# FFN up projection as seven block products (Strassen's scheme, Winograd's form), FFN in two phases through DRAM

## The chip, the cores and the metric

The kernel runs on one core of one Trainium2 chip. The metric is the device time of one execution in microseconds (us). The engines are TensorE (PE in the profile, its weight loads PEld), VectorE (DVE), ScalarE (ACT), GpSimd (POOL) and SyncE (SP), which here only issues DMAs. Every engine works through its own instructions in order and waits on semaphores for the others.

## The reference, cut to what matters

One layer of a model trunk: 1024 tokens, width 1024, FFN width 2816, all in fp32. The change lies in the gated FFN with its causal convolution of width 3, and in the residual around it:

```
h2 = rmsnorm(x, g_ffn[i])
u = causal_dwconv(h2 @ w_up[i], conv_w[i], conv_b[i])          # w_up: 1024 x 5632
x = x + (jax.nn.gelu(u[..., :D_FF], approximate=True) * u[..., D_FF:]) @ w_down[i]   # 2816 x 1024
ple_gate = jax.nn.sigmoid(rmsnorm(x, g_ple[i]) @ w_ple_gate[i])
x = x + ple_gate * (p[i] @ w_ple_up[i])
```

## The kernel before, in words

Every fp32 operand of a product is split into a high part (fp32r, rounded by a ScalarE cast) and the rest (a VectorE subtraction); `split` does both. A product is then three matmuls: high x high, high x rest, rest x high. Each matmul here multiplies a 128x128 stationary block with 128x512 moving columns.

Mixer output. `wout` multiplies the merged branches with the four column quarters of `w_out` and adds them to the eight 128-token rows of x1 (`self.x1[tb]`, in SBUF). In the loop for quarters 2 and 3, `norm_rows` makes the normed rows and `turn` transposes one (8 transposes of 128x128 in two PSUM banks, each emptied by one cast and one subtraction) into `hT`: `ha` for tokens 0 to 511, `hb` for 512 to 1023, each with a high and a rest tile.

Up projection (`ffn`). For each of 22 blocks f, two 128-column blocks of `w_up` are loaded and split: block f (the gelu half) and block 22 + f (the linear half). `gemmT` multiplies one with one token half: 8 contraction blocks x 3 matmuls. So f costs 2 x 2 x 24 = 96 matmuls. `conv` reads the 128x1024 PSUM result: one ScalarE activation and two VectorE multiply-adds on shifted columns. Then gelu, a product of the halves, and a split into `mh`, `ml`.

Down projection (`down`). After two f, their 256 rows of `w_down` are multiplied with every token row: 12 matmuls per row, in two PSUM tiles `ps` of 128x512 (there are two such buffers), each added into x1 by VectorE. This work lies between the up projections of the next f. The last three f are multiplied in the loop that also norms x1 for the last gate (`ple`).

The program fixes the order in which tiles are allocated; a scheduler then sets each engine's order, which is why the orders below are printed from the built programs.

## Time and profile before

| | us |
|---|---|
| median of 3 runs | 1943.54 (1942.53 to 1951.27) |
| the profiled execution | 1945.69 |
| its span, first to last instruction | 1944.0 |
| TensorE busy in the span | 1892.3 (97%) |
| VectorE busy | 1026.9 (53%) |
| ScalarE busy | 686.8 (35%) |
| GpSimd busy | 102.0 (5%) |

The span is the profiled execution without the 1.7 us around it. Busy shares are sums over stages with different limits; a stage is read by its own window, and there by which engine waits for which.

### The profile page before, as it was taken

How to read it: one execution, taken by the hardware profiler on the slowest of the kernel's cores; microseconds unless marked ns; L12 is line 12 of the kernel's file. 1: busy time of each engine (PE TensorE's matmuls, PEld its weight loads, DVE VectorE, ACT ScalarE, POOL GpSimd, SP SyncE). 2: the span in 40 equal slices, each digit the busy share in tenths (PEclk: the TensorE clock that was granted, in tenths of full speed). 3: DMA queues.
4: the chain of work that ended last, by engine and by line, in shares of the span. 5: the costliest groups of instructions: out<-in, count | busy, mean ns of one | idle time of the engine just before them, and what ended most of it. 6: DMA issues, size and time to landing. Idle time of an engine off the chain costs nothing.

```text
span 1944.0 us, 27675 instructions
## 1 busy us (share of the span) xinstructions
PE 1892.3 (97%) x11215; PEld 1550.3 (80%) x11215; DVE 1026.9 (53%) x2193; ACT 686.8 (35%) x1069; POOL 102.0 (5%) x99
## 2 busy tenths in 40 slices
...
GB/s 154 87 152 152 146 133 94 70 75 46 72 32 82 136 118 146 129 133 92 260 169 74 55 55 44 45 43 55 47 35 60 50 49 33 62 26 54 27 148 55
DMA packets 249766, 169.75 MB, mean 87 GB/s; under 512 B 76488, under 2 KB 226718, under 8 KB 249639
## 3 DMA queue, kind: packets, MB, share of 16 engines
...
## 4 chain that ended last, share of the span: by engine, by line
PE 67%; DMA 2%; ACT 1%; DVE 1%; issue 1%; POOL 0%; ACTq 0%; SPq 0%; POOLq 0%; DVEq 0%
PE zt L235 10%; PE zt L236 10%; PE zt L237 10%; PE ps L228 4%; PE ps L227 4%; PE ps L226 4%; PE zt L226 3%; PE zt L227 3%; PE zt L228 3%; PE zt L985 2%; PE zt L987 2%; PE zt L986 1%; PE yps L635 1%; PE yps L648 1%; DMA vr<-in_w_out 1%; PE tr L842 1%
## 5 line engine op out<-in xcount | busy, mean ns | idle before, releaser
L207 DVE TENSOR_TENSOR wl<-wr,wh 128x1024 fp32r<-128x1024 f32 (+1 forms) x78 | 91.0, 1168 | 248.9 <-ACT wh L206 248.5
L235 PE MATMUL zt<-hah,wh 128*128 128x512 f32 (+1 forms) x552 | 219.8, 399 | 0.0
L235 PE MATMUL zt<-hbh,wh 128*128 128x512 f32 (+1 forms) x552 | 218.1, 395 | 0.2 <-ACT hbh L285 0.2
L236 PE MATMUL zt<-hal,wh 128*128 128x512 f32 (+1 forms) x552 | 218.1, 395 | 0.0
L236 PE MATMUL zt<-hbl,wh 128*128 128x512 f32 (+1 forms) x552 | 217.7, 394 | 0.0
L237 PE MATMUL zt<-hbh,wl 128*128 128x512 f32 (+1 forms) x552 | 217.3, 394 | 0.0
L237 PE MATMUL zt<-hah,wl 128*128 128x512 f32 (+1 forms) x552 | 217.0, 393 | 0.0
L206 ACT CAST wh<-wr 128x1024 fp32r<-128x1024 f32 (+1 forms) x87 | 84.2, 970 | 346.3 <-PE zt L236 299.1
L1065 DVE TENSOR_TENSOR x<-x,ps 128x512 f32<-128x512 f32 x154 | 105.3, 686 | 96.0 <-PE ps L228 94.8
L226 PE MATMUL ps<-vh,mh 128*128 128x512 f32 (+1 forms) x334 | 128.7, 385 | 0.2 <-DVE x L1042 0.2
L228 PE MATMUL ps<-vh,ml 128*128 128x512 f32 (+1 forms) x334 | 128.6, 385 | 0.0
L227 PE MATMUL ps<-vl,mh 128*128 128x512 f32 (+1 forms) x334 | 128.5, 385 | 0.0
L235 PEld LDWEIGHTS zt<-hah,wh 128*128 128x128 f32 x552 | 104.6, 190 | 23.8 <-issue 0.5
L235 PEld LDWEIGHTS zt<-hbh,wh 128*128 128x128 f32 x552 | 104.3, 189 | 23.7 <-ACT hbh L285 0.5
L236 PEld LDWEIGHTS zt<-hal,wh 128*128 128x128 f32 x552 | 104.6, 189 | 23.3 <-issue 1.0
L236 PEld LDWEIGHTS zt<-hbl,wh 128*128 128x128 f32 x552 | 104.3, 189 | 23.5 <-DVE hbl L286 0.4
L237 PEld LDWEIGHTS zt<-hah,wl 128*128 128x128 f32 x552 | 104.5, 189 | 23.3 <-issue 0.2
L237 PEld LDWEIGHTS zt<-hbh,wl 128*128 128x128 f32 x552 | 104.5, 189 | 23.1
L206 ACT CAST vh<-vr 128x1024 fp32r<-128x1024 f32 x34 | 34.1, 1047 | 209.3 <-PE ps L228 178.0
L226 PEld LDWEIGHTS ps<-vh,mh 128*128 128x128 f32 x334 | 63.0, 189 | 13.6 <-DVE x L1042 0.4
L227 PEld LDWEIGHTS ps<-vl,mh 128*128 128x128 f32 x334 | 63.0, 189 | 13.4
L228 PEld LDWEIGHTS ps<-vh,ml 128*128 128x128 f32 x334 | 63.0, 188 | 13.3
(395 smaller groups left out, 4073.3 us busy)
## 6 DMA issues: line engine op xcount, KB each, us to landing
wr<-in_w_up SPq DMA_DIRECT2D x44, 512.0 KB
...
wr<-in_w_in ACTq DMA_DIRECT2D x21, 512.0 KB
gwr<-in_w_in ACTq DMA_DIRECT2D x11, 512.0 KB
xt<-in_x SPq DMA_DIRECT2D x8, 512.0 KB
...
fwr<-in_w_in ACTq DMA_DIRECT2D x8, 512.0 KB
```

The lines of the kernel that those rows point to most:

```text
L206: self.nc.scalar.copy(h, r)
L207: eng.tensor_sub(l, r, h.bitcast(F32))
L226: nc.tensor.matmul(ps, lhsT=lh, rhs=rh, start=(i == 0), stop=False)
L227: nc.tensor.matmul(ps, lhsT=lh, rhs=rl, start=False, stop=False)
L228: nc.tensor.matmul(ps, lhsT=ll, rhs=rh, start=False, stop=(i == n - 1))
L235: nc.tensor.matmul(o, lhsT=H[:, k, :], rhs=hh[:, k, :], start=(k == 0), stop=False)
L236: nc.tensor.matmul(o, lhsT=H[:, k, :], rhs=hl[:, k, :], start=False, stop=False)
L237: nc.tensor.matmul(o, lhsT=L[:, k, :], rhs=hh[:, k, :], start=False, stop=(k == NKB - 1))
L635: mm(yps[i][r, o], lhsT=X[r, i, k, :], rhs=main(X, i, X_R)[r], start=True, stop=False)
L985: nc.tensor.matmul(ps[:, cs], lhsT=H[:, k, :], rhs=yh[:, k, cs], start=(k == 0), stop=False)
L987: nc.tensor.matmul(ps[:, cs], lhsT=L[:, k, :], rhs=yh[:, k, cs], start=False, stop=(k == 3))
L1065: self.nc.vector.tensor_add(self.x1[tb][:, cs], self.x1[tb][:, cs], ps)
```

## The change

The up projection of block f is treated as a 2x2 block product. The rows of the left matrix are the gelu block and the linear block (A1., A2.), its columns the lower and the upper 512 of the contraction; the right matrix has the same halves of the contraction as rows and the two token halves as columns (B.1, B.2). Seven products of 12 matmuls take the place of eight. Their operands are sums: s1 = a21 + a22, s2 = s1 - a11, s3 = a11 - a21, s4 = a12 - s2 on the weights (`up_s12`, `up_s3`: four GpSimd operations of 128x512 for each f), and t1 to t4 on the tokens (`up_norm`: four GpSimd operations for each pair of token rows, once). Only token rows 0 to 3 go through `turn`; t1 to t4 and b22 are transposed by `up_turn` (5 x 4 transposes for each pair). The results are put together in SBUF tiles c0 (gelu half) and c1 (linear half) by one copy and seven adds from PSUM, and `up_conv` reads these. x1 is normed in place, after a copy to DRAM (`x1d`). The gated rows go to DRAM (`md`). After all 22 f, x1 is loaded again, and `ffn_down` reads `md` and `w_down` for group after group of two f.

```diff
+    def up_norm(self, p, tmp):
+
+
+        xa, xb = self.x1[p], self.x1[p + 4]
+        lo, hi = slice(0, 512), slice(512, 1024)
+        sub = self.nc.gpsimd.tensor_sub
+        t2 = tmp.tile([P, 512], F32, name="t2", tag="t2", bufs=4)
+        sub(xa[:, lo], xb[:, lo], xa[:, lo])
+        sub(t2, xb[:, hi], xa[:, lo])
+        sub(xb[:, lo], xb[:, hi], xb[:, lo])
+        sub(xa[:, hi], xa[:, hi], t2)
+        return dict(t1=xa[:, lo], t2=t2, t3=xb[:, lo], t4=xa[:, hi], b22=xb[:, hi])
...
+    def up_turn(self, p, rows, pools):
+
+        nc = self.nc
+        ts = slice(p * P, p * P + P)
+        for n, op in enumerate(("t2", "t1", "t3", "t4", "b22")):
+            ps = pools()
+            for k in range(4):
+                nc.tensor.transpose(ps[:, k * P:k * P + P], rows[op][:, k * P:k * P + P], self.ident)
+            p3 = ps[:].rearrange("p (k t) -> p k t", t=P)
+            H, L = self.B[op]
+            nc.scalar.copy(H[:, :, ts], p3)
+            nc.vector.tensor_sub(L[:, :, ts], p3, H[:, :, ts].bitcast(F32))
+            yield 0.44
...
+    def up_s12(self, f):
+
+        r0, r1 = self.raws[f]
+        A, gp = self.A[f], self.nc.gpsimd
+        A["s1"], A["s2"] = self.up_tile("vr")
+        s1, s2, s4 = [self.up.tile([P, 4, P], F32, name=n, tag=n, bufs=1) for n in ("s1r", "s2r", "s4r")]
+        gp.tensor_add(s1, r1[:, 0:4], r1[:, 4:8])
+        gp.tensor_sub(s2, s1, r0[:, 0:4])
+        gp.tensor_sub(s4, r0[:, 4:8], s2)
+        self.sums[f] = s1, s2, s4
...
+    def up_mul(self, ps, f, w, b):
+        nc = self.nc
+        (wh, wl), (bh, bl) = self.A[f][w], self.B[b]
+        for k in range(4):
+            nc.tensor.matmul(ps, lhsT=wh[:, k, :], rhs=bh[:, k, :], start=k == 0, stop=False)
+            nc.tensor.matmul(ps, lhsT=wh[:, k, :], rhs=bl[:, k, :], start=False, stop=False)
+            nc.tensor.matmul(ps, lhsT=wl[:, k, :], rhs=bh[:, k, :], start=False, stop=k == 3)
+            yield 0.7
...
+    def up_m(self, f, c0, u1):
+        nc = self.nc
+        u0 = self.up_conv(c0, f)
+        nc.scalar.activation(u0, u0, AF.Gelu_apprx_tanh)
+        nc.vector.tensor_mul(u0, u0, u1)
+        nc.sync.dma_start(self.md[f], u0)
...
+            m1 = mul(f, "a11", "b11") if f else first[0]
+            nc.scalar.copy(c0[:, lo], m1)
+            if f:
+                u1 = self.up_conv(before[1], NFB + f - 1)
+            else:
+                self.up_load(1)
+            m2 = mul(f, "a12", "b21") if f else first[1]
+            if f:
+                self.up_m(f - 1, before[0], u1)
+                self.up_rest(f)
+            m6 = mul(f, "s2", "t2")
+            add(c0[:, hi], c0[:, lo], m6)
+            add(c0[:, lo], c0[:, lo], m2)
+            if f + 2 < NFB:
+                self.up_load(f + 2)
+            m5 = mul(f, "s1", "t1")
+            if more:
+                self.up_a1(f + 1)
+                self.up_s12(f + 1)
+            else:
+                last()
+            m7 = mul(f, "s3", "t3")
+            add(c1[:, lo], c0[:, hi], m7)
+            add(c1[:, hi], c1[:, lo], m5)
+            add(c0[:, hi], c0[:, hi], m5)
+            if more:
+                self.up_halve(self.A[f + 1]["s2"], self.sums[f + 1][1][:])
+                self.up_halve(self.A[f + 1]["s1"], self.sums[f + 1][0][:])
+            m4 = mul(f, "a22", "t4")
+            add(c1[:, lo], c1[:, lo], m4)
+            m3 = mul(f, "s4", "b22")
+            if more:
+                self.up_s3(f + 1)
+            add(c0[:, hi], c0[:, hi], m3)
+            before = c0, c1
+        u1 = self.up_conv(before[1], 2 * NFB - 1)
+        self.up_m(NFB - 1, before[0], u1)
...
+    def ffn_down(self, ms, pools):
+
+        for g in range(1, NFB // 2):
+            raws = self.down_load(g)
+            for tb in range(NTB):
+                if g == NFB // 2 - 1:
+                    self.down(ms[:1], tb, self.zt.tile([P, T], F32, name="zt", tag="zt") if tb % 2 else None)
                 else:
-                    before = ms
-        return before[1:] + ms
+                    self.down(ms, tb)
+                if tb == 2:
+                    after = self.down_split(g, raws, pools)
+            ms = ms[1:] + after if g == NFB // 2 - 1 else after
+        return ms
...
+
+        def scale(tb):
+            x = self.x1[tb]
+            nc.vector.scalar_tensor_tensor(x, x, scales[tb], g, op0=ALU.mult, op1=ALU.mult)
+        for i in range(NTB + 3):
+            if i < NTB:
+                self.wout(m, 2, W2, order[i], z_tile)
+            if i >= 3:
+                tb = order[i - 3]
+                self.wout(m, 3, W3, tb, z_tile)
+                self.dump("x1", self.x1[tb], tb)
+                scales[tb] = self.rms_scale(self.x1[tb], junk, tmp)
+                nc.sync.dma_start(self.x1d[tb], self.x1[tb])
+            if i >= 4:
+                scale(order[i - 4])
+            if i in (5, 7, 9):
+                self.turn(order[i - 5], self.x1[order[i - 5]], [hT])
+            if i == 5:
+                self.up_a1(0)
+            if i in (6, 8, 10):
+                sums.append(self.up_norm(i // 2 - 3, tmp))
...
+        def norm2():
+            w = self.up_first(junk)
+            self.turn(3, self.x1[3], [hT])
+            next(w)
+            yield 0.88
+            yield from self.up_turn(0, sums[0], t_tile)
+            scale(7)
+            sums.append(self.up_norm(3, tmp))
+            next(w)
+            yield from self.up_turn(1, sums[1], t_tile)
+            next(w)
+            yield from self.up_turn(2, sums[2], t_tile)
+            run(w)
+            yield from self.up_turn(3, sums[3], t_tile)
+        first = [self.pu.tile([P, 512], F32, name="pu", tag="pu") for _ in range(2)]
+        interleave((norm2(), 9.7), (flat([[0.9], self.up_mul(first[0], 0, "a11", "b11"),
+                                          self.up_mul(first[1], 0, "a12", "b21")]), 6.5))
...
+        self.ffn_up(first, lambda: ms.extend(self.down_first(hA)))
+        close_up()
+        close_h2()
+        close_ps()
+        close_ps = self.pools(("ps", 2), ("zt", 3))
+        xp1, _ = self.pool("x1", side="right")
+        self.x1 = [xp1.tile([P, D], F32, name=f"x1_{tb}") for tb in reversed(range(NTB))][::-1]
+        for tb in range(NTB):
+            nc.sync.dma_start(self.x1[tb], self.x1d[tb])
...
+        ms = self.ffn_down(ms, [(hA, "hah"), (hA, "hal"), (hB, "hbh"), (hB, "hbl")])
```

**Order 1.** VectorE, one f of the up projection. Before, for one f: the split of the weights, the two multiply-adds of each half (they read PSUM, `zt`), the product and the split.

```order
L207 TENSOR_TENSOR wl_12044<-wr_12041,wh_12043 128x1024 [waits DMAHW7_49,PE_49,Activation_49]
L1053 SCALAR_TENSOR_TENSOR uc_11964<-zt_11915,par_111,uc_11964 128x1023 [waits Activation_49]
L1054 SCALAR_TENSOR_TENSOR uc_11964<-zt_11915,par_111,uc_11964 128x1022 [waits DVE_49]
L207 TENSOR_TENSOR wl_12231<-wr_12228,wh_12230 128x1024 [waits DMAHW1_49,PE_49,Activation_49]
L1053 SCALAR_TENSOR_TENSOR uc_12023<-zt_11974,par_111,uc_12023 128x1023 [waits Activation_49]
L1054 SCALAR_TENSOR_TENSOR uc_12023<-zt_11974,par_111,uc_12023 128x1022 [waits DVE_49]
L1096 TENSOR_TENSOR uc_11964<-uc_11964,uc_12023 128x1024 [waits DVE_49]
L207 TENSOR_TENSOR ml_12030<-uc_11964,mh_12029 128x1024 [waits Activation_49]
```

In the change, for one f, the stretch from the sixth product (m4) to the product with the linear half; the operations before it are the other adds and the subtractions for s2 and s1.

```order
L1216 TENSOR_TENSOR c1_11611<-c1_11611,pu_11718 128x512 [waits DVE_49,PE_49]
L1100 TENSOR_TENSOR vh_11745<-s3r_11746,vh_11745 128x512 [waits Activation_49]
L1100 TENSOR_TENSOR vh_11745<-rr_11531,vh_11745 128x512 [waits DMAHW5_49,Activation_49]
L1162 SCALAR_TENSOR_TENSOR u_11767<-c1_11611,par_111,u_11767 128x1023 [waits Activation_49]
L1220 TENSOR_TENSOR c0_11610<-c0_11610,pu_11732 128x512 [waits PE_49]
L1163 SCALAR_TENSOR_TENSOR u_11767<-c1_11611,par_111,u_11767 128x1022 [waits DVE_49]
L1100 TENSOR_TENSOR vl_11793<-s4r_11694,vl_11793 128x512 [waits Activation_49]
L1162 SCALAR_TENSOR_TENSOR u_11784<-c0_11610,par_111,u_11784 128x1023 [waits DMAHW2_49,Activation_49]
L1163 SCALAR_TENSOR_TENSOR u_11784<-c0_11610,par_111,u_11784 128x1022 [waits DVE_49]
L1090 TENSOR_TENSOR wl_11970<-rr_11811,wh_11969 128x1024 [waits DMAHW1_49,PE_49,Activation_49]
L1170 TENSOR_TENSOR u_11784<-u_11784,u_11767 128x1024 [waits Activation_49]
L1198 TENSOR_TENSOR c0_11751<-c0_11751,pu_11796 128x512 [waits PE_49]
```

And GpSimd for one f, which had no work in this stage before:

```order
L1108 TENSOR_TENSOR s1r_11692<-rr_11531 128x512 [waits DMAHW5_49,DVE_49]
L1109 TENSOR_TENSOR s2r_11693<-s1r_11692,rr_11529 128x512 [waits DMAHW3_49,Pool_49]
L1119 TENSOR_TENSOR s3r_11746<-rr_11529,rr_11531 128x512 [waits DVE_49]
L1110 TENSOR_TENSOR s4r_11694<-rr_11529,s2r_11693 128x512 [waits DVE_49,Pool_49]
```

What moved: the multiply-adds read SBUF (c1_11611 and c0_11610, the tiles c1 and c0 of this f) instead of PSUM, three subtractions of 128x512 and the one of 128x1024 stand among them, and GpSimd makes four sums beside them.

**Order 2.** VectorE between the loop of `wout` and the first product with a sum. x1_7 is the last row to be finished; `t2l`, `t4l`, `b22l`, `vl` are the rest tiles of the transposed sums, `vr` those of s1 and s2, `vl_10602` that of s4 (from `wh_9994`, made by GpSimd).

```order
L1072 TENSOR_TENSOR b22l_10577<-pu_10640,b22h_10576 128x4x128 [waits Activation_49]
L1072 TENSOR_TENSOR vl_10585<-ps_10623,vh_10584 128x4x128 [waits Activation_49,Pool_49]
L1575 SCALAR_TENSOR_TENSOR x1_7_9522<-x1_7_9522,nst_10548,wl_9992 128x1024 [waits DMAHW3_49,DVE_49]
L1100 TENSOR_TENSOR vr_10603<-wh_9994,vr_10603 128x512 [waits Pool_49]
L1072 TENSOR_TENSOR t2l_10581<-ps_10656,t2h_10580 128x4x128 [waits Activation_49]
L1072 TENSOR_TENSOR t1l_10583<-pu_10666,t1h_10582 128x4x128 [waits Activation_49]
L1072 TENSOR_TENSOR vl_10585<-pu_10673,vh_10584 128x4x128 [waits Activation_49]
L1072 TENSOR_TENSOR t4l_10579<-ps_10680,t4h_10578 128x4x128 [waits Activation_49]
L1072 TENSOR_TENSOR b22l_10577<-pu_10690,b22h_10576 128x4x128 [waits Activation_49]
L1100 TENSOR_TENSOR vr_10603<-wh_9994,vr_10603 128x512 [waits Pool_49]
L1100 TENSOR_TENSOR vl_10602<-wh_9994,vl_10602 128x512 [waits Activation_49]
L1072 TENSOR_TENSOR t2l_10581<-pu_10701,t2h_10580 128x4x128 [waits PE_49]
```

What moved: where `turn` of one row (two subtractions) stood beside 24 matmuls, there are now twenty subtractions for the sums, the scaling of x1_7 in their midst, and the first product that uses a sum (t2) needs the last of the four t2l, seven rows below these.

**Order 3.** SyncE's DMAs. Before, in the middle of the FFN:

```order
L215 DMA vr_12033<-in_w_down 128x2x1024 [waits DMAHW6_49,DVE_49]
L215 DMA wr_11844<-in_w_up 128x8x128 [waits DMAHW1_49,DVE_49]
L215 DMA wr_11909<-in_w_up 128x8x128 [waits DMAHW2_49,DVE_49]
L215 DMA wr_11968<-in_w_up 128x8x128 [waits DMAHW4_49,DVE_49]
L215 DMA wr_12041<-in_w_up 128x8x128 [waits DMAHW5_49,DVE_49]
```

In the change, at the end of the up projection; `u_13863` is the last gated row, `vr` the raw tile of `w_down`, of which there is one.

```order
L1171 DMA md_9999<-u_13754 128x1024 [waits DVE_49]
L1254 DMA vr_13908<-in_w_down 128x2x1024 [waits DMAHW1_49,PE_49]
L1254 DMA vr_14053<-in_w_down 128x2x1024 [waits DMAHW1_49,DVE_49]
L1171 DMA md_9999<-u_13863 128x1024 [waits DMAHW3_49,DVE_49]
L1254 DMA vr_14198<-in_w_down 128x2x1024 [waits DMAHW4_49,DMAHW2_49,DVE_49]
L1644 DMA x1_0_13890<-x1d_9998 128x1024 [waits DMAHW6_49,DMAHW5_49]
L1644 DMA x1_1_13889<-x1d_9998 128x1024
```

VectorE at the same place: the splits of `vr_13908` and `vr_14053`, the end of the last convolution, and the first adds of the down projection.

```order
L207 TENSOR_TENSOR vl_13963<-vr_13908,vh_13962 128x1024 [waits DMAHW1_49,Activation_49]
L207 TENSOR_TENSOR vl_13963<-vr_13908,vh_13962 128x1024 [waits Activation_49]
L1220 TENSOR_TENSOR c0_13721<-c0_13721,pu_13845 128x512 [waits DVE_49,PE_49]
L1162 SCALAR_TENSOR_TENSOR u_13859<-c1_13722,par_111,u_13859 128x1023 [waits Activation_49]
L1163 SCALAR_TENSOR_TENSOR u_13859<-c1_13722,par_111,u_13859 128x1022 [waits DVE_49]
L1162 SCALAR_TENSOR_TENSOR u_13863<-c0_13721,par_111,u_13863 128x1023 [waits DMAHW0_49,Activation_49]
L1163 SCALAR_TENSOR_TENSOR u_13863<-c0_13721,par_111,u_13863 128x1022 [waits DVE_49]
L207 TENSOR_TENSOR vl_14108<-vr_14053,vh_14107 128x1024 [waits DMAHW2_49,Activation_49]
L1170 TENSOR_TENSOR u_13863<-u_13863,u_13859 128x1024 [waits Activation_49]
L207 TENSOR_TENSOR vl_14108<-vr_14053,vh_14107 128x1024 [waits Activation_49]
L1233 TENSOR_TENSOR x1_0_13890<-x1_0_13890,ps_13914 128x512 [waits DMAHW5_49,PE_49]
L1233 TENSOR_TENSOR x1_0_13890<-x1_0_13890,ps_13922 128x512 [waits PE_49]
```

What moved: the loads of x1 stand behind the third load of `w_down`, which waits for the split of the second, which stands on VectorE behind the last convolution.

## Rows read from the trace of the kernel before

**Rows 1.** The page's first line.

```profile
span 1944.0 us, 27675 instructions
```

**Rows 2.** Windows: the FFN's 22 up projections, then the rest of the kernel.

```profile
core 0: us, PE busy (x) PEld busy (x) DVE busy (x) ACT busy (x) POOL busy (x), PEclk, DMA share, GB/s
1098.47:1796.84 698.37, 698.13 (x3010) 563.25 (x3009) 341.55 (x365) 166.16 (x168) 0.00 (x0) 1.00 0.16 48
1796.84:1944.00 147.16, 142.59 (x1025) 132.85 (x1023) 83.75 (x168) 42.51 (x83) 4.55 (x6) 0.99 0.23 76
```

**Rows 3.** Groups by line and shape, TensorE, in the first of these windows.

```profile
L235 PE MATMUL zt<-hah,wh 128*128 128x512 f32 x352 | 139.4, 396 | 0.0
...
L226 PE MATMUL ps<-vh,mh 128*128 128x512 f32 x288 | 114.2, 396 | 0.0
```

**Rows 4.** Timeline of TensorE: start, us, engine, line, operation.

```profile
1099.17 1.04 PE L283 MATMUL ps<-ident,nx 128*128 128x128 f32 x8
1099.97 0.48 PE L235 MATMUL zt<-hah,wh 128*128 128x512 f32 x1
```

**Rows 5.** Groups by shape, VectorE, 1060 us to the end: busy, mean ns | idle before.

```profile
L1065 DVE TENSOR_TENSOR x<-x,ps 128x512 f32<-128x512 f32 x154 | 105.3, 686 | 96.0 <-PE ps L228 94.8
...
L1053 DVE SCALAR_TENSOR_TENSOR uc<-zt,par,uc 128x1023 f32<-128x1023 f32 x44 | 56.2, 1277 | 3.6 <-ACT uc L1052 3.6
L207 DVE TENSOR_TENSOR wl<-wr,wh 128x1024 fp32r<-128x1024 f32 x44 | 53.9, 1225 | 225.9 <-ACT wh L206 225.9
...
L1096 DVE TENSOR_TENSOR uc<-uc 128x1024 f32<-128x1024 f32 x22 | 27.0, 1225 | 0.7
...
L286 DVE TENSOR_TENSOR hal<-ps,hah 128x512 fp32r<-128x512 f32 x16 | 10.3, 685 | 1.4 <-ACT hah L285 1.3
```

**Rows 6.** The same for ScalarE.

```profile
L206 ACT CAST wh<-wr 128x1024 fp32r<-128x1024 f32 x44 | 46.1, 1049 | 213.2 <-PE zt L236 213.2
...
L1095 ACT ACTIVATE uc<-uc 128x1024 f32<-128x1024 f32 x22 | 23.3, 1061 | 62.1 <-DVE uc L1054 62.1
...
L285 ACT CAST hah<-ps 128x512 fp32r<-128x512 f32 x16 | 8.8, 589 | 15.7 <-PE ps L283 15.4
```

**Rows 7.** Timeline of VectorE near the kernel's start.

```profile
18.27 3.27 DVE L1208 SCALAR_TENSOR_TENSOR nx<-xt,nst,g 128x1024 f32<-128x1024 f32 x1
21.47 1.28 DVE L286 TENSOR_TENSOR hal<-ps,hah 128x512 fp32r<-128x512 f32 x2
...
30.59 1.27 DVE L1208 SCALAR_TENSOR_TENSOR nx<-xt,nst,g 128x1024 f32<-128x1024 f32 x1
```

**Rows 8.** Timeline of GpSimd, there and near 990 us.

```profile
18.09 2.37 POOL L207 TENSOR_TENSOR wl<-wr,wh 128x1024 fp32r<-128x1024 f32 x1 [2.85 <-ACT wh L206]
...
987.56 2.28 POOL L207 TENSOR_TENSOR wl<-wr,wh 128x512 fp32r<-128x512 f32 x1
991.46 1.28 POOL L207 TENSOR_TENSOR wl<-wr,wh 128x512 fp32r<-128x512 f32 x1 [1.62 <-ACT wh L206]
```

**Rows 9.** Timeline of SyncE: two loads of 1024 KB, the first issued at 1854.96.

```profile
1854.96 9.03 SPq L215 DMA_DIRECT2D vr<-in_w_ple_gate  x2
```

**Rows 10.** Timeline of ScalarE: the casts of that first load.

```profile
1860.14 2.00 ACT L206 CAST vh<-vr 128x1024 fp32r<-128x1024 f32 x2 [1.85 <-DMA vr<-in_w_ple_gate]
```

**Rows 11.** DMA issues: size, median us from issue to landing.

```profile
x<-in_x POOLq DMA_DIRECT2D x8, 384.0 KB, 9.3
...
out<-ml POOLq DMA_DIRECT2D x6, 512.0 KB, 4.1
```

**Rows 12.** Windows (columns as in Rows 2): a burst of loads, and around an idle TensorE.

```profile
1012.00:1018.00 6.00, 6.00 (x55) 6.00 (x55) 0.84 (x2) 0.00 (x0) 0.54 (x1) 1.00 1.05 395
...
285.00:289.00 4.00, 0.59 (x3) 0.15 (x1) 3.69 (x12) 1.53 (x2) 0.00 (x0) 1.00 0.88 215
...
293.00:297.00 4.00, 4.00 (x13) 4.00 (x14) 2.24 (x13) 1.63 (x3) 0.01 (x1) 0.50 1.04 326
...
298.00:299.00 1.00, 1.00 (x7) 1.00 (x7) 0.00 (x0) 0.00 (x0) 0.00 (x0) 1.00 0.98 213
```

**Rows 13.** Timeline of VectorE: one of the adds of a down projection.

```profile
1306.66 0.69 DVE L1065 TENSOR_TENSOR x<-x,ps 128x512 f32<-128x512 f32 x1 [0.71 <-PE ps L228]
```

More of the change, by code (lines that the diff above doesn't have):

```diff
@@ new lines, in up_s3, with up_first @@
+    def up_s3(self, f, r=None):
+        r0, r1 = self.raws[f]
+        A = self.A[f]
+        A["s3"], A["a22"] = self.up_tile("vh")
+        if r is None:
+            r = self.up.tile([P, 4, P], F32, name="s3r", tag="s3r", bufs=1)
+        self.nc.gpsimd.tensor_sub(r, r0[:, 0:4], r1[:, 0:4])
+        self.up_halve(A["s3"], r)
+    def up_first(self, junk):
+        r0, r1 = self.raws[0]
+        A, gp = self.A[0], self.nc.gpsimd
+        A["s4"] = self.up_tile("vl")[0]
+        A["s1"], A["s2"] = self.up_tile("vr")
+        a, b = [junk[:, i:i + 512].rearrange("p (k n) -> p k n", n=P) for i in (0, 512)]
+        gp.tensor_add(a, r1[:, 0:4], r1[:, 4:8])
+        gp.tensor_sub(b, a, r0[:, 0:4])
+        yield
+        self.up_halve(A["s1"], a)
+        gp.tensor_sub(a, r0[:, 4:8], b)
+        yield
+        self.up_halve(A["s2"], b)
+        self.up_halve(A["s4"], a)
+        yield
+        self.up_s3(0, b)
+        self.up_halve(A["a22"], r1[:, 4:8])
@@ new lines, in up_m, with ffn_up, mul @@
+    def up_m(self, f, c0, u1):
[4 more added lines that the diff above has]
+        nc.sync.dma_start(self.md[f], u0)
+    def ffn_up(self, first, last):
+        nc, up, add = self.nc, self.up, self.nc.vector.tensor_add
+        lo, hi = slice(0, 512), slice(512, 1024)
+        def mul(f, w, b):
+            ps = self.pu.tile([P, 512], F32, name="pu", tag="pu")
+            run(self.up_mul(ps, f, w, b))
+            return ps
+        before = None
+        for f in range(NFB):
+            more = f + 1 < NFB
+            c0 = up.tile([P, T], F32, name="c0", tag="c0", bufs=2)
+            c1 = up.tile([P, T], F32, name="c1", tag="c1", bufs=2)
+            m1 = mul(f, "a11", "b11") if f else first[0]
[35 more added lines that the diff above has]
+        self.up_m(NFB - 1, before[0], u1)
@@ new lines, in down_first @@
+    def down_first(self, pool):
+        nc = self.nc
+        M = pool.tile([P, 4, T], F32R, name="hah", tag="hah", bufs=1)
+        ms = []
+        for f in range(2):
+            W = self.wload(self.a["w_down"][f * P:f * P + P, :])
+            raw = self.up.tile([P, T], F32, name="rr", tag="rr", bufs=2)
+            nc.sync.dma_start(raw, self.md[f])
+            mh, ml = M[:, 2 * f], M[:, 2 * f + 1]
+            self.split(raw, mh, ml)
+            ms.append(((mh, ml), (W[0][:, 0, :], W[1][:, 0, :])))
+        return ms
```

160 lines of the change are left out of this document (88 added, 72 removed).

## The prediction

> **What bounds the kernel now.** I read the page's first line, the windows, then the groups by line and the timelines of the engines at the places where the order changes. The span is 1944.0 us [rows 1]. In the stage that the change rebuilds, 698.37 us of it, TensorE is busy for 698.13 at the full clock, VectorE for half, ScalarE for a quarter, GpSimd not at all [rows 2]. So TensorE alone sets this stage's length, and the reader should see that what the other engines do there is free only as long as TensorE waits for none of them. The stage holds 2976 matmuls of 128x512 (six groups like the first of [rows 3], three like the second) and four rows of transposes, 0.80 us each [rows 4]: (698.37 - 3.2) / 2976 = 0.2336 us from one matmul to the next. A down projection's add takes 0.69 us, and VectorE then waits 0.71 us for the next PSUM tile [rows 13]: that is the room other work has beside it.
>
> **What is removed and added on TensorE.** 2112 matmuls of the up projection become 22 x 7 x 12 = 1848: 264 x 0.2336 = 61.7 us less. Transposes rise from 64 to 32 + 80 = 112: 48 x 0.10 = 4.8 us more. The down projection keeps its 1056 matmuls.
>
> **One f of the up projection.** TensorE needs 84 x 0.2336 = 19.6 us (2.80 for each product). VectorE has seven adds (0.686), four multiply-adds (1.277), five subtractions of 128x512 (0.685), one of 128x1024 and one product (1.225 each) [rows 5]: 4.8 + 5.1 + 3.4 + 2.5 = 15.8 us. ScalarE has some 8 (gelu 1.06, a cast 1.05, halves 0.59 [rows 6]). Does the order fit? The sixth product, m4, ends 16.8 us into f. From there the rows of Order 1 take 0.7 + 1.4 + 1.3 + 0.7 + 1.3 + 0.7 + 2.6 + 2.5 = 11.2 us; gelu lies beside the 128x1024 subtraction. Two adds make it 29.4; the next row waits for m5 of the next f, at 19.6 + 11.2 = 30.8. So 1.4 us are spare, and 0.8 more before m7. Into this stretch GpSimd puts s3 and s4. Near the start a multiply-add with two SBUF inputs took 3.27 us instead of 1.27 while GpSimd worked, but a subtraction from PSUM kept its 0.64 [rows 7, 8]. A GpSimd sum of 128x512 takes 1.28 us, or 2.28 in company [rows 8]. Two of them cost VectorE up to 2.6 us, 1.2 more than is spare; the wait before m7 takes 0.8, and since weights for the next f are ready a product or more ahead and six PSUM tiles lie between the engines, I count nothing. If that cover is gone, each us is paid 21 times.
> The Trainium skill speaks against the change here: its page GPSIMD Engine Reference (Specifications) says that GpSimd shares SBUF interfaces with VectorE and contends with VectorE instructions that have two SBUF inputs. The 3.27 us agree with it; I make it a rival below.
>
> **First joint: from `wout` to the first product with a sum.** TensorE's own work after the last `wout` product is 24 matmuls and 88 transposes: 5.6 + 8.8 = 14.4 us. VectorE starts scaling x1_3 some 2.0 us after that product (the last add, and the copy to DRAM that has to land first, 4.1 us after its issue [rows 11]). Up to the rest tile of the last t2 it has 23 subtractions (0.64 in a row [rows 7]) and two scalings (1.27): 2.0 + 14.7 + 2.5 = 19.2. In between it waits for s4: x1_7 is scaled at 9.0, GpSimd then makes four sums and s4 (5 x 1.28) and ScalarE casts, 16.0, while VectorE is there at 14.1: 1.9 lost. Five of its operations have two SBUF inputs with GpSimd busy beside them; half a sum each is 3.2. Together 24.3, so TensorE stands for 24.3 - 14.4 = 10 us where it stood for nothing. Bounds: 5 (no GpSimd waits), 18 (sums of 2.28, every conflict in full).
>
> **Second joint: from the up to the down projection.** Time 0 is the end of the last product. The raw tile `vr` is free when m5 ends, at -8.4. A load of 1024 KB takes 5.2 us to its cast [rows 9, 10], so the first split ends at about 0.4 (two casts, two subtractions). The second load then lands at 5.6. VectorE meanwhile does the last add and four multiply-adds, to 6.2; then comes one subtraction of the second split (7.9), the product (9.1; gelu stood behind the cast), the other subtraction (10.3). Only then does SyncE issue the third load, and behind it x1's first row (Order 3): 1.5 MB at 395 GB/s [rows 12] are 4.0 us, and 2.5 are what the 5.2 us hold besides the data, so with the issues the row lands at 17.3 and the first add ends at 18.0. TensorE has two PSUM tiles, 2.8 us of work: it stands for 15.3 us. Afterwards eight subtractions (9.8 us) stand among ten adds that leave 7.1: 2.7 lost. And the clock: after an idle of nearly 4 us the granted clock was 0.50, the 1.2 GHz level, for about 5 us of work, then full again [rows 12]; half of that is 2.3. Together 20 us. Bounds: 10, if the loads overlap better, and 28, if two loads wait like the queued ones of 9.3 us [rows 11].
> [...]
>
> **Down projection alone.** Before, splits lay beside up projections, where VectorE was idle. Now four subtractions (4.9 us) stand among the first adds of a group, whose five gaps hold 3.6; with the spare PSUM tile about 1 us is lost, in four groups (the other groups have two subtractions there): 4 us, bounds 0 and 8. The reloads (2 MB in 22 us) are far below the rate of [rows 12]. The copies of x1 and `md` to DRAM cost nothing beyond the two joints: SyncE issues them, and the up projection's 1.5 MB per 19.6 us are a fifth of that rate. The last stage keeps its work [rows 2].
>
> **Sum.** -61.7 + 4.8 + 10 + 20 + 4 = -22.9 us. The profiled execution took 1945.7 (the span and 1.7 us around it), 2.2 above the median of the runs; so 1923 against it and **1921 us** against the median. The terms' bounds give -42 and -3, that is 1902 to 1941.
>
> **Rivals.**
> 1. The joints are short: loads and sums lie mostly beside TensorE's work, 5 + 10 + 0: 1902 us or less. For it: the burst rate of 395 GB/s. Against: Order 3 puts three waits in a row. Chance 0.10.
> 2. VectorE becomes the bound of the up projection because all four sums of f hold it: 15.8 + 4 x 1.28 = 20.9 us, 1.3 x 21 = 27 us more: 1948. For it: [rows 7]; against: s1 and s2 fall beside adds from PSUM. Chance 0.11.
> 3. The slower one: VectorE is the bound and also stands, in every f, for gelu (1.06) and a cast (0.59), since the chain no longer waits for TensorE but for ScalarE: 22.5 us, 2.9 x 21 = 61 more: 1982. It decides from 21.1 us per f on (32 us over 21 f). For it: the multiply-adds and the product are one chain over two engines; against: Order 1 puts another operation beside gelu. Chance 0.08.
> 4. The change doesn't save what it says, since each of 154 shorter products pays a start: at 0.2 us that is 31 us, 1952. Against: groups of 6 and of 24 matmuls alternate in the stage at one rate [rows 2, 3]. Chance 0.05.
>
> **How the numbers follow.** My forecast, TensorE as the bound with two long joints, has 0.66; its own range is 1905 to 1938. A measurement of this kernel can tell about 0.5% from no change, here 1933.8 and 1953.3. Faster: nearly all of the forecast and rival 1, 0.71. Same: a little of the forecast, most of rivals 2 and 4, 0.16. Slower: rival 3 and the tails of 2 and 4, 0.13. The range for 8 in 10, 1902 to 1950, takes in the forecast, half of rival 1 and most of rival 2.
>
> **What would show it.** In the up projection, TensorE should be busy without gaps, a period of f of 19.6 us, VectorE busy about 85%. Rivals 2 and 3 would show as gaps before products, released by VectorE, and multiply-adds well over 1.28 us. At the first joint, transposes should wait for VectorE, about 10 us in all. At the second, TensorE should stand once for 13 to 18 us until an x1 row lands, with SyncE waiting for a VectorE subtraction before it, and show a clock of 0.5 afterwards. The prediction is wrong in its largest term if the matmuls follow each other at another distance than 0.2336, and in its joints if the x1 loads are issued early.

## The result, and the profile after

The changed kernel takes 1927.05 us (median of four runs, 1923.34 to 1927.56) where the kernel before takes 1944.63 (also of four): a ratio of 0.9900, with a 95% interval of 0.9872 to 0.9927, or 17.6 us less. In two later sets it was 0.9904 (0.9890 to 0.9917) and 0.9903 (0.9884 to 0.9922). The forecast was 1921, with a range of 1902 to 1950. The profiled execution took 1923.34 us, the shortest of the four:

```profile
span 1921.6 us, 28252 instructions
PE 1841.3 (96%) x10999; PEld 1506.5 (78%) x10999; DVE 1213.8 (63%) x2447; ACT 746.9 (39%) x1191; POOL 264.4 (14%) x203
```

Windows of the changed kernel, which answer to [rows 2]: from the last `wout` product to the first product with a sum, the up phase, the turn to the down phase, the down phase, the last stage.

```profile
core 0: us, PE busy (x) PEld busy (x) DVE busy (x) ACT busy (x) POOL busy (x), PEclk, DMA share, GB/s
1097.67:1125.71 28.04, 19.22 (x114) 16.20 (x112) 23.37 (x40) 16.12 (x32) 15.92 (x12) 0.88 0.26 76
1125.71:1550.09 424.38, 424.38 (x1824) 341.42 (x1825) 358.59 (x392) 173.62 (x218) 135.20 (x84) 1.00 0.27 85
1550.09:1567.78 17.69, 2.96 (x13) 2.08 (x12) 10.15 (x11) 4.18 (x4) 0.00 (x0) 0.70 0.63 223
1567.78:1797.00 229.22, 224.39 (x953) 178.01 (x954) 153.72 (x207) 42.07 (x45) 0.00 (x0) 0.99 0.28 100
1797.00:1921.60 124.60, 119.07 (x925) 114.31 (x923) 65.42 (x138) 35.83 (x73) 4.55 (x6) 1.00 0.24 81
```

The reader is to see that TensorE is busy for the whole up phase, 424.38 us of 424.38 for 1824 matmuls: 0.2327 us each, against 0.2336 before. VectorE is at 84% there. The long stands lie in the two joints. Where TensorE stands there, in its timeline (the bracket is the idle time before the row and what ended it):

```profile
1103.03 1.94 PE L283 MATMUL ps<-ident,x 128*128 128x128 f32 x8 [2.62 <-DVE nst L262]
...
1120.38 1.12 PE L1068 MATMUL pu<-ident,x 128*128 128x128 f32 x4 [3.51 <-DVE t2l L1072]
...
1125.71 0.50 PE L1152 MATMUL pu<-t2h,vr 128*128 128x512 f32 x1 [1.22 <-ACT c L1188]
...
1567.78 0.80 PE L226 MATMUL ps<-wh,hah 128*128 128x512 f32 x1 [14.73 <-DVE x L1233]
```

The second joint reads as the prediction's Order 3 has it. SyncE's timeline: the first two loads of `w_down`, the last gated row, the third load, and only then x1.

```profile
1541.94 8.92 SPq L1254 DMA_DIRECT2D vr<-in_w_down  x2
1559.10 0.34 SPq L1171 DMA_DIRECT2D md<-u  x1
1560.24 0.37 SPq L1254 DMA_DIRECT2D vr<-in_w_down  x1
1560.70 5.28 SPq L1644 DMA_DIRECT2D x<-x1d  x8
```

VectorE's timeline beside it: the last split, then an idle of 6.82 us until the first row of x1 has landed.

```profile
1558.99 1.22 DVE L207 TENSOR_TENSOR vl<-vr,vh 128x1024 fp32r<-128x1024 f32 x1
1567.04 1.28 DVE L1233 TENSOR_TENSOR x<-x,ps 128x512 f32<-128x512 f32 x2 [6.82 <-DMA x<-x1d]
```

One f of the up phase, the four multiply-adds on VectorE, which answer to the 1.277 us of [rows 5]:

```profile
1178.61 1.86 DVE L1162 SCALAR_TENSOR_TENSOR u<-c,par,u 128x1023 f32<-128x1023 f32 x1 [0.37 <-ACT u L1161]
...
1180.99 1.27 DVE L1163 SCALAR_TENSOR_TENSOR u<-c,par,u 128x1022 f32<-128x1022 f32 x1
...
1182.78 1.27 DVE L1162 SCALAR_TENSOR_TENSOR u<-c,par,u 128x1023 f32<-128x1023 f32 x1
1184.09 2.20 DVE L1163 SCALAR_TENSOR_TENSOR u<-c,par,u 128x1022 f32<-128x1022 f32 x1
```

and GpSimd's sums, s3 and s4 in the same stretch, s1 and s2 behind it:

```profile
1177.71 1.68 POOL L1119 TENSOR_TENSOR s3r<-wr 128x512 f32<-128x512 f32 x1 [2.28 <-DVE vh L1100]
1183.00 2.21 POOL L1110 TENSOR_TENSOR s4r<-wr,s2r 128x512 f32<-128x512 f32 x1 [3.62 <-DVE vl L1100]
1192.31 1.29 POOL L1108 TENSOR_TENSOR s1r<-rr 128x512 f32<-128x512 f32 x1 [7.10 <-DVE vr L1100]
1193.68 1.29 POOL L1109 TENSOR_TENSOR s2r<-s1r,rr 128x512 f32<-128x512 f32 x1
```

Two of the four multiply-adds take 0.59 and 0.93 us longer; the other two keep 1.27, although one of them (1182.78) lies beside s4 as well. By these rows the two engines take turns: s4 begins inside that multiply-add, which ends at 1184.05, and ends 1.16 us after it; the next multiply-add begins at 1184.09 and ends 1.08 us after s4. Each waits for the one that began before it, and GpSimd's 2.21 us hold some 0.9 of waiting. The last two rows are s1 and s2, with VectorE's adds from PSUM beside them: 1.29 us each.

### The profile page after: what moved, and what is told of

The parts are those of the page before. It is cut to its first block, busy times and chain, and to the rows that moved or that the text cites. A ratio compares the mean times of both kernels' runs of the same rounds, so it can differ in the third digit from the quotient of the medians.

```text
span 1921.6 us, 28252 instructions
## 1 busy us (share of the span) xinstructions
PE 1841.3 (96%) x10999; PEld 1506.5 (78%) x10999; DVE 1213.8 (63%) x2447; ACT 746.9 (39%) x1191; POOL 264.4 (14%) x203
## 4 chain that ended last, share of the span: by engine, by line
PE 61%; DVE 5%; DMA 2%; ACT 2%; issue 2%; POOL 0%; SPq 0%; DVEq 0%; ACTq 0%; POOLq 0%
PE pu L1152 7%; PE pu L1153 7%; PE pu L1154 7%; PE zt L228 3%; PE zt L226 3%; PE ps L226 3%; PE zt L227 3%; PE ps L228 3%; PE ps L227 3%; PE zt L985 2%; PE zt L987 2%; PE zt L235 2%; PE zt L236 2%; PE zt L986 2%; PE zt L237 2%
## 5 line engine op out<-in xcount | busy, mean ns | idle before, releaser
L235 PE MATMUL zt<-hah,wh 128*128 128x512 f32 (+1 forms) x200 | 80.4, 403 | 0.0
L236 PE MATMUL zt<-hal,wh 128*128 128x512 f32 (+1 forms) x200 | 78.8, 394 | 0.0
L235 PE MATMUL zt<-hbh,wh 128*128 128x512 f32 (+1 forms) x200 | 78.7, 393 | 0.0
L237 PE MATMUL zt<-hah,wl 128*128 128x512 f32 (+1 forms) x200 | 77.8, 389 | 0.0
L236 PE MATMUL zt<-hbl,wh 128*128 128x512 f32 (+1 forms) x200 | 77.7, 389 | 0.0
L237 PE MATMUL zt<-hbh,wl 128*128 128x512 f32 (+1 forms) x200 | 77.7, 388 | 0.0
L1163 DVE SCALAR_TENSOR_TENSOR u<-c,par,u 128x1022 f32<-128x1022 f32 x44 | 74.5, 1694 | 0.8
L1152 PE MATMUL pu<-hah,wh 128*128 128x512 f32 x176 | 70.6, 401 | 0.0
L1153 PE MATMUL pu<-hal,wh 128*128 128x512 f32 x176 | 69.7, 396 | 0.0
L1154 PE MATMUL pu<-hah,wl 128*128 128x512 f32 x176 | 69.6, 395 | 0.0
L848 DVE TENSOR_TENSOR pl<-tr,ph 128x512 fp32r<-128x512 f32 (+1 forms) x80 | 50.0, 633 | 14.4 <-ACT ph L847 13.9
L207 DVE TENSOR_TENSOR wl<-wr,wh 128x1024 fp32r<-128x1024 f32 (+1 forms) x36 | 39.5, 1100 | 24.7 <-ACT wh L206 24.3
```

The lines of the kernel that those rows point to most:

```text
L235: nc.tensor.matmul(o, lhsT=H[:, k, :], rhs=hh[:, k, :], start=(k == 0), stop=False)
L236: nc.tensor.matmul(o, lhsT=H[:, k, :], rhs=hl[:, k, :], start=False, stop=False)
L237: nc.tensor.matmul(o, lhsT=L[:, k, :], rhs=hh[:, k, :], start=False, stop=(k == NKB - 1))
L1152: nc.tensor.matmul(ps, lhsT=wh[:, k, :], rhs=bh[:, k, :], start=k == 0, stop=False)
L1153: nc.tensor.matmul(ps, lhsT=wh[:, k, :], rhs=bl[:, k, :], start=False, stop=False)
L1154: nc.tensor.matmul(ps, lhsT=wl[:, k, :], rhs=bh[:, k, :], start=False, stop=k == 3)
```

## The experiments

All runs are compared inside their set. Where a set has no run of the changed kernel, its ratio of 0.9904 to the kernel before stands in, with 1945 us for that kernel; the interval of that ratio, 0.9890 to 0.9917, is 2.6 us either way.

**The yardstick.** The changed kernel, unaltered, in the first and the last set.

> The changed kernel once more, unaltered, as the yardstick for the others and for a second look at its spread: three of its four executions took 1926.9 to 1927.6 us, the profiled one 1923.3. Theory: the difference is clock, since the mean granted clock was 0.985 to 0.986 there and 0.988 in the profile, which is 8 to 12 us more at the 1.2 GHz level, worth 4 to 6 us. Then the median is again about 1926 and an execution near 1923 shows 0.988. Rival: the difference is a wait of another length (a DMA), and clock and time do not go together.

> The changed kernel unaltered, as the yardstick of this set: 0.990 of the kernel before.

Measured: 1925.47 us (1924.32 to 1926.46) and 1927.41 us (1920.69 to 1929.29). Over the 14 runs, time and mean granted clock go together: 1920.7 at 0.989, 1923.3 at 0.988, 1924.3 to 1928.1 at 0.986 and 0.987, 1926.1 to 1929.3 at 0.985. The theory on the spread holds that far; that the clock is the cause isn't shown by it, since the clock also falls after a wait. Where it falls is taken up below.

**Loads of x1 on another queue.**

```diff
-        self.x1 = [xp1.tile([P, D], F32, name=f"x1_{tb}") for tb in reversed(range(NTB))][::-1]
+        x1 = {tb: xp1.tile([P, D], F32, name=f"x1_{tb}") for tb in (6, 7, 0, 1, 2, 5, 3, 4)}
+        self.x1 = [x1[tb] for tb in range(NTB)]
         for tb in range(NTB):
-            nc.sync.dma_start(self.x1[tb], self.x1d[tb])
+            nc.gpsimd.dma_start(self.x1[tb], self.x1d[tb])
```

> The eight loads of x1 leave SyncE for GpSimd's DMA queue, and its rows lie where tiles of the up phase become free first, so that no load of w_down stands ahead of them. Theory (the second joint hangs on SyncE's order, then on VectorE's): the first add of x1 moves from 17.0 us after the last product to about 10.2, where VectorE is done with the last convolution and the splits; TensorE's long stand falls from 14.7 to about 8 us, and the kernel gains 6 to 7 us. Rival 1 (only the transfer counts, not its place): the loads take some 9 us on that queue, as x did near the start, and the gain is under 3 us. Rival 2 (given back): the loads of the gated rows then come first and TensorE waits later; no gain.

Measured: 1931.56 us, 6.1 slower than the yardstick. My theory missed. TensorE's timeline in this run:

```profile
1563.35 0.79 PE L226 MATMUL ps<-wh,hah 128*128 128x512 f32 x1 [9.65 <-DVE x L1233]
...
1580.46 0.80 PE L226 MATMUL ps<-wh,hah 128*128 128x512 f32 x1 [11.99 <-DVE x L1233]
```

and VectorE's:

```profile
1562.61 1.28 DVE L1233 TENSOR_TENSOR x<-x,ps 128x512 f32<-128x512 f32 x2
1578.58 1.22 DVE L207 TENSOR_TENSOR hal<-uc,hal 128x1024 fp32r<-128x1024 f32 x1 [14.69 <-ACT hal L206]
1579.72 0.68 DVE L1233 TENSOR_TENSOR x<-x,ps 128x512 f32<-128x512 f32 x1
```

The first stand shrank from 14.9 to 9.7 us, not to 8, since the first load of `w_down` now shared the way with x1's first row and its split came 2 us later. But on VectorE the split of the first gated rows now stands before the second row's add, and those rows were issued at 1563.14, behind seven rows of x1 (3.5 MB) and a load of `w_down`: it was cast only at 1577.50. With the rows themselves that is 5.5 MB, and at the 395 GB/s of [rows 12] 14.6 us; 14.4 passed, at this rate:

```profile
1563.00:1577.00 14.00, 5.12 (x12) 3.71 (x12) 0.89 (x2) 0.00 (x0) 0.00 (x0) 0.62 1.01 380
```

Rival 2 is what happened: the loads of the joint are one burst, and a queue that lets one part ahead makes another late.

**More PSUM for the first group.**

```diff
-                    self.down(ms, tb)
+                    self.down(ms, tb, self.zt.tile([P, T], F32, name="zt", tag="zt") if g == 1 and tb in (1, 2, 3) else None)
```

> Rows 1 to 3 of the first group of the down projection go into the three 128x1024 PSUM tiles, which are there and idle, instead of the two of 128x512; the DMAs stay as they are. Theory (TensorE stands because two PSUM tiles hold only 2.8 us of work until the first row of x1 is there): TensorE works 11.2 us before it stands, and stands about 6 us instead of 14.7; gain 8 to 10 us. Rival 1 (VectorE, not PSUM): the three larger adds (1.28 us each) and the splits pile up behind the first row, and half of it is given back: 3 to 5 us. Rival 2: the PSUM tiles of the last products are not free early enough, no gain.

Measured: 1917.84 us, 7.6 less than the yardstick, just under the theory's 8 to 10 and above rival 1. TensorE stands 6.71 us where it stood 14.94, and its stands before the third group come to 1.8 us, as they did (1.9):

```profile
1569.20 0.80 PE L226 MATMUL ps<-wh,hah 128*128 128x512 f32 x1 [6.71 <-DVE x L1233]
```

The DMAs are where they were; 8.4 us more work in PSUM hid 8.2 us of waiting.

**s4 in a tile of its own.**

```diff
+        c = s4[:].rearrange("p (k n) -> p k n", n=P)
+        gp.tensor_sub(c, r0[:, 4:8], b)
         yield
         self.up_halve(A["s1"], a)
-        gp.tensor_sub(a, r0[:, 4:8], b)
         yield
         self.up_halve(A["s2"], b)
-        self.up_halve(A["s4"], a)
+        self.up_halve(A["s4"], c)
...
-            w = self.up_first(junk)
+            w = self.up_first(junk, tmp.tile([P, 512], F32, name="s4", tag="s4", bufs=1))
```

> First joint: the sum s4 of the first block gets a tile of its own, so that GpSimd makes it before the four sums of the last pair of rows and not behind them. Theory: VectorE's wait of 3.0 us for it in the midst of the subtractions goes, TensorE's stand of 3.5 us shrinks by as much, and with it the clock's fall that followed (about 1.6 us); gain 3 to 4.5 us. Rival: the last pair of rows is what is late (x1_7 scaled at 11.6 us into the joint, then its sums until 17.7), the wait only moves to its transposes, gain under 1.5 us.

Measured: 1921.51 us, 4.0 less. The sum is made at 1105.98, ahead of the last pair's four sums, instead of at 1116.57 behind them, and the stand of 3.5 us is 0.70, with the clock full after it:

```profile
1119.38 0.66 PE L1068 MATMUL pu<-ident,x 128*128 128x128 f32 x4 [0.70 <-DVE t2l L1072]
```

After the earlier stand of 2.62 us the clock stayed at 0.5 longer than in the change (over the ten us from 1102 on it is 0.66 here and 0.83 there), so that the clock lost as much in this one fall, 3.4 us, as in the change's two: by the traces the joint is 2.7 us shorter (25.3 us from the last `wout` product to the first with a sum), the stand's part alone. The rest of the 4.0 is not told apart from the spread.

**Two phases without the seven products.** All eight rows are turned, no sums are made, and each f has four results of 24 matmuls.

```diff
-            m6 = mul(f, "s2", "t2")
...
+            nc.scalar.copy(c0[:, lo], mul(f, "a1", "1") if f else first[0])
...
+            nc.scalar.copy(c0[:, hi], mul(f, "a1", "2"))
...
+                nc.scalar.copy(c1[:, lo], mul(f, "a2", "1"))
...
+            nc.scalar.copy(c1[:, hi], mul(f, "a2", "2"))
```

> One part alone: the FFN in two phases with the gated rows and x1 in DRAM stays, but the up projection is eight plain products (96 matmuls for each f, no sums of weights or tokens, all eight rows turned). Theory (TensorE bounds the up phase, seven products save what they leave out): a period of 22.3 us for each f, 61 us more in the phase; the first joint loses its waits of some 13 us and the 48 transposes (5 us), so the kernel is 40 to 46 us slower than the change, 1965 to 1972, which is 22 to 29 us over the kernel before: the price of the two phases by themselves. Rival (the change's up phase pays for its sums somewhere, so that the seven products save less): the difference to the change is under 30 us.

Measured: 1974.46 us, a ratio of 1.0145 (1.0131 to 1.0159) to the kernel before, 28 us over it and 47 over the change, a little more than the 40 to 46 expected. One f of this kernel in the windows:

```profile
1190.00:1212.33 22.33, 22.33 (x98) 17.98 (x97) 8.46 (x7) 7.51 (x10) 0.00 (x0) 1.00 0.23 71
```

22.33 against 19.54 us: 2.8 us for each f, exactly the twelve matmuls left out. So the sums cost the up phase nothing; the rival is out. The two phases alone cost 28 us, of which the stand at the second joint, 15.29 us here, is the largest piece.

**More work for VectorE.** The rest of a 128x1024 block is made two or four times (n = 2, 4).

```diff
-        self.nc.vector.tensor_sub(L, r0, H[:].bitcast(F32))
+        for _ in range(n if f else 1):
+            self.nc.vector.tensor_sub(L, r0, H[:].bitcast(F32))
```

> In the change, VectorE makes the rest of the 128x1024 weights twice in every f after the first: 1.22 us more work, the result is the same. Theory (TensorE is the bound; in a period of 19.54 us VectorE is busy for 16.55, so 3.0 are spare): no change, within 3 us. Rival (VectorE's chain of operations is already what the products wait for at some place, although it has idle time elsewhere): every us is paid 21 times, 15 to 26 us slower.

> The same with three repetitions, 3.66 us more for each f. Theory: VectorE then needs 20.2 us, 0.7 more than TensorE, so that the period becomes 20.2 us or a little more (its waits for a product's end can't all be used): 14 to 30 us slower, TensorE waiting before products for VectorE. Rival 1 (as for one repetition, a fixed chain): 45 us slower or more. Rival 2 (more is spare than the profile shows, since multiply-adds that share with GpSimd get shorter): no change.

Measured: with one repetition 1926.89 us, ratio 0.9901: no change. With three 1936.21 us, ratio 0.9948, some 9 us slower: less than the 14 to 30 expected. Windows of one f early in the up phase, and of 20 us late in it:

```profile
1200.00:1219.54 19.54, 19.54 (x86) 15.72 (x85) 19.54 (x22) 7.65 (x11) 8.24 (x4) 1.00 0.24 72
1430.00:1450.00 20.00, 19.96 (x85) 15.61 (x84) 19.77 (x22) 7.55 (x10) 7.38 (x4) 1.00 0.25 80
```

VectorE has no idle time left, yet TensorE keeps its 19.54 us until the ninth f; only then does the period become 20.0. VectorE's lag, some 0.45 us in each f, first has to use up what lies between the engines (products in PSUM, weights made ahead; how much each of them holds isn't shown). The rest is paid at the end: the second joint's stand is 20.35 us.

**Sums on VectorE.** From the second f on, `nc.vector` instead of `nc.gpsimd` in `up_s12` and `up_s3`.

> In the change, from the second f on, the four sums of weights are made by VectorE instead of GpSimd. Theory (the multiply-adds' means of 1.55 and 1.71 us instead of 1.28 come from GpSimd's sums beside them): they are back at 1.28, VectorE gains 4 x 0.69 and loses 1.5 us for each f, 17.8 of 19.5 us busy, and the time is the change's within 3 us. Rival (they are longer because they read SBUF and not PSUM): they stay at their means, VectorE is at 19.3 us, and the kernel is slower by 3 us or more.

Measured: 1924.07 us, ratio 0.9895 beside the yardstick's 0.9903: no change. Groups of the multiply-adds from 1150 to 1540 us (busy us, mean ns), first in the unaltered kernel of this set,

```profile
L1163 DVE SCALAR_TENSOR_TENSOR u<-c,par,u 128x1022 f32<-128x1022 f32 x41 | 70.7, 1724 | 0.7
L1162 DVE SCALAR_TENSOR_TENSOR u<-c,par,u 128x1023 f32<-128x1023 f32 x40 | 62.1, 1553 | 7.5 <-ACT u L1161 7.5
```

then here:

```profile
L1162 DVE SCALAR_TENSOR_TENSOR u<-c,par,u 128x1023 f32<-128x1023 f32 x40 | 51.1, 1278 | 0.4 <-ACT u L1161 0.4
L1163 DVE SCALAR_TENSOR_TENSOR u<-c,par,u 128x1022 f32<-128x1022 f32 x40 | 51.1, 1277 | 0.0
```

So it is GpSimd beside them, not the SBUF source, that made them long. This is the rule of the Trainium skill (GPSIMD Engine Reference, Specifications) that the prediction weighed; the rows agree with it, 1.72 against 1.28 us.

**Both joints.** s4's tile, the PSUM tiles, x1 and the first two gated rows on GpSimd's queue, and the pool of the up phase laid out so that x1 falls on tiles that are free early.

```diff
-        for tag, n, bufs in (("u", T, 2), ("s1r", 512, 1), ("s2r", 512, 1), ("s4r", 512, 1), ("s3r", 512, 1),
-                             ("c0", T, 2), ("c1", T, 2), ("rr", T, 2)):
+        for tag, n, bufs in (("s1r", 512, 1), ("s2r", 512, 1), ("s4r", 512, 1), ("s3r", 512, 1),
+                             ("rr", T, 2), ("c0", T, 2), ("c1", T, 2), ("u", T, 2)):
...
-            self.nc.sync.dma_start(raws[-1], self.md[f])
+            (self.nc.gpsimd if g <= 1 else self.nc.sync).dma_start(raws[-1], self.md[f])
```

> Both joints shortened: s4's own tile (first joint); three PSUM tiles of 128x1024 for rows 1 to 3 of the first group; the loads of x1 and of the first group's gated rows on GpSimd's DMA queue, x1 in tiles that become free before the last product ends, so that on VectorE all adds of the first group stand ahead of the splits. Theory (the second joint was SyncE's order, then VectorE's): the first add moves to 10.2 us after the last product, TensorE stands 3 us there or less; 1906 to 1911. Rival 1 (the early loads take bandwidth from w_down's load, which delays its split and all that stands behind it on VectorE, as with the loads on that queue alone): TensorE stands 5 us or more, 1912 to 1916. Rival 2 (given back in the next group): TensorE waits again after 23 us for the splits, 1915 or more.

Measured: 1910.40 us, a ratio of 0.9816 (0.9802 to 0.9829): 36 us faster than the kernel before, 17 than the change, within the theory's 1906 to 1911. VectorE now makes the first group's adds ahead of the gated rows' splits, from 12.1 us after the last product on; the 2 us over the 10.2 are again the wait for the first load of `w_down`. What is left of the stands:

```profile
1560.37 0.51 PE L226 MATMUL ps<-wh,hah 128*128 128x512 f32 x1 [1.49 <-DVE x L1234]
...
1564.96 0.50 PE L226 MATMUL ps<-wh,hah 128*128 128x512 f32 x1 [1.54 <-DVE x L1234]
...
1577.20 0.47 PE L226 MATMUL ps<-vh,hal 128*128 128x512 f32 x1 [3.72 <-ACT hal L206]
```

**The last x1 row back on SyncE**, to take away the 3.72 us; the edit is against the version above.

```diff
-            nc.gpsimd.dma_start(self.x1[tb], self.x1d[tb])
+            (nc.gpsimd if tb < 7 else nc.sync).dma_start(self.x1[tb], self.x1d[tb])
```

> As the version with both joints shortened, but the last of the eight x1 loads goes back to SyncE, so that the loads of the first gated rows on GpSimd's queue don't stand behind it (it had waited there until 1566.4 us for a tile). Theory: TensorE's stand of 3.7 us before the second group goes, 20 to 22 us faster than the change (17 were without this). Rival (the rows would have been late anyway, since 3 MB of other loads are under way): the stand stays above 2 us, 17 to 18.5 us faster than the change.

Measured: 1913.37 us, ratio 0.9839 (0.9821 to 0.9858), 14 faster than the yardstick: no gain over the version above, and less than the rival's 17 to 18.5. TensorE stands 1.92 us before and 3.22 us at the start of the second group. Counted from the last product (1547.53 above, 1551.05 here), the two rows were issued at 11.8 and 12.3 us instead of 19.4 and 19.9, but the cast of the first begins at 23.5 instead of 26.6 and that of the second at 28.4, as above (28.5). For the first row the rival holds: of the 7.6 us by which it is issued earlier 3.1 are left, the burst takes the rest. The second row is held up elsewhere. On ScalarE its cast (the third line) comes after that of a row of the next group, which waits for its own load:

```profile
1574.52 1.05 ACT L206 CAST hal<-uc 128x1024 fp32r<-128x1024 f32 x1 [12.99 <-DMA uc<-md]
1578.53 1.04 ACT L206 CAST hbh<-uc 128x1024 fp32r<-128x1024 f32 x1 [2.96 <-DMA uc<-md]
1579.48 1.04 ACT L206 CAST hal<-uc 128x1024 fp32r<-128x1024 f32 x1
```

And that load SyncE now issued behind the last x1 row, at 1570.38 (19.3 us after the last product instead of 12.6):

```profile
1569.99 0.34 SPq L1645 DMA_DIRECT2D x<-x1d  x1
1570.38 11.93 SPq L1258 DMA_DIRECT2D uc<-md  x4
```

So both the burst and a place in a queue, now SyncE's, make the rows late.

## Why the prediction was right, point by point

**TensorE bounds the up phase: right.** The period of f is 19.54 us (19.6 forecast), a product is 2.80 us as its twelve matmuls are, so no product pays a start, and rival 4 is out. 1848 x 0.2327 against 2112 x 0.2336 is some 63.3 us less; the term was 61.7.

**VectorE has room: right.** It is busy 358.59 us in 424.38, 16.5 for each f, where 15.8 were added up. Of the up to 2.6 us for GpSimd's sums, 1.5 came, from s3 and s4 as the text had it (the rows' durations overlap by some 0.08 us at each step, so that they add up to more than the busy time). Rivals 2 and 3 needed 20.9 and 22.5 us, and TensorE never waited there. One repetition more was free, three were not, so the room is real: between 1.2 and 3.7 us by these runs, 3.0 by the busy time.

**The first joint: right in mechanism, its size too small.** 24.3 us were forecast from the last `wout` product to the first with a sum, 28.04 came. The stands are 1.48 + 2.62 + 3.51 + 1.22 = 8.8 us, near the 10, and on VectorE they come about as forecast: five of its operations take 3.9 us longer beside GpSimd's sums (3.2 forecast), and it waits 3.04 us for s4 (1.9), since x1_7 is scaled at 11.6 us instead of 9.0. The rows, of which the fourth is the scaling of x1_7 and the others are the five (0.16, 0.16, 1.28, 0.68 and 0.68 us without GpSimd):

```profile
1098.16 1.20 DVE L246 TENSOR_TENSOR nst<-nst 128x1 f32<-128x1 f32 x1
...
1099.80 0.80 DVE L248 TENSOR_TENSOR nst<-nst 128x1 f32<-128x1 f32 x1
1100.63 2.25 DVE L1575 SCALAR_TENSOR_TENSOR x<-x,nst,wl 128x1024 f32<-128x1024 f32 x1
...
1109.28 1.28 DVE L1575 SCALAR_TENSOR_TENSOR x<-x,nst,wl 128x1024 f32<-128x1024 f32 x1
...
1114.06 1.41 DVE L1100 TENSOR_TENSOR vr<-wh,vr 128x512 fp32r<-128x512 f32 x1
1118.51 1.21 DVE L1100 TENSOR_TENSOR vl<-wh,vl 128x512 fp32r<-128x512 f32 x1 [3.04 <-ACT vl L1099]
```

The term that is missing from the sum is the clock: after the stands of 2.62 and of 3.51 us the granted clock was at 0.5, the 1.2 GHz level, as windows of the change show:

```profile
1103.00:1107.00 4.00, 3.97 (x18) 3.56 (x19) 2.78 (x8) 2.39 (x6) 2.34 (x2) 0.57 0.00 0
1120.00:1124.00 4.00, 3.62 (x16) 3.23 (x17) 4.00 (x8) 2.60 (x5) 0.00 (x0) 0.57 0.97 265
```

8 us at 0.57 are 3.4 us of work lost. The other 1.4 lie where transposes and matmuls alternate: at the full clock the matmul behind a group of four transposes takes 0.32 us until the next one starts, not 0.23, and some of the groups 0.43, not 0.40. A stand of 1.23 us in the loop of `wout`, before a turn, wasn't in the sum either. The experiment with s4 shows the part of it that was one operation's place in a queue: 2.7 us by the traces, 4.0 by the medians.

**The second joint: right.** Stand 14.73 us (15.3 forecast), x1's first row issued 10.6 us after the last product and added from 16.95 on (17.3), later stands 0.90 + 0.56 + 1.37 = 2.8 (2.7). Only the clock was too dear: six matmuls took 2.73 us instead of 1.40, 1.3 lost, where I took half of 5 us.

**Splits in the down phase: smaller.** Six stands of 0.25 us, 1.5, where 4 were forecast, and 1.1 us once in the last stage, where the kernel before stood 0.4.

**The sum.** From the last `wout` product on, the change takes 823.9 us (1097.67 to 1921.6) and the kernel before 845.5 (from the start of [rows 2], 1098.47, to 1944.0): 21.6 us less; the whole of the two profiled executions differs by 22.4, and 22.9 were forecast. That the sum comes this close is in part luck: the first joint costs 3.6 us more than forecast and the products save some 1.6 more, while the second joint and the splits cost 1.1 and 1.8 less. The medians differ by only 17.6 to 18. What separates them from the profiled executions lies ahead of the change: in three profiles of the changed kernel the time from the first turn in the last `wout` loop to the end is 847.8, 849.0 and 847.7 us (868.8 in the kernel before, 19.8 to 21.1 more), while that turn starts at 1073.83, 1075.77 and 1077.40. In the stages before that loop, with the same code in both kernels, the clock falls in other places from run to run: from 220 to 240 us it is 1.00 in the first of these profiles and 0.91 in the second, from 680 to 700 us 0.91 and 0.83. No trace shows them longer in the changed kernel: in the twelve profiles of kernels that share its code up to that turn, it starts at 1073.83 to 1078.64, 1075.6 in the mean, and in the one profile of the kernel before at 1075.17. A difference of a microsecond or two in the mean can't be excluded with one profile, so the last 2 to 3 us between the traces and the medians stay open.

**That two joints would take back half of the saving** is what the experiment with eight products shows from the other side: the seven products gain 47 us, with what their sums cost at the first joint already taken off, and 28 us are paid for the two phases.
